# Mean over 8192 rows: two more row groups loaded as a pair, and a different split of one group between TensorE and VectorE

## The chip, the cores and the metric

The kernel runs on one core of one Trainium2 chip. A core has TensorE (matrix multiply, into PSUM banks), VectorE (called DVE in the profile), ScalarE (ACT), GpSimd (POOL), SyncE (SP, which here only issues transfers and waits), and sixteen DMA engines that move data between HBM and the on-chip SBUF. The metric is the device time of one execution in microseconds (us), lower being better. Before the change it was 628.19 us, the median of three runs that went from 628.13 to 628.68.

## The reference

```python
def setup_inputs():
    return {"x": np.random.randn(8192, 8192).astype(np.float32)}

def reference(x):
    return np.mean(x, axis=0)
```

The input is 8192 x 8192 float32, 268.4 MB, and each element is needed once. The output is 8192 means, one per column.

## The kernel before, in words

The rows are cut into 64 groups of 128 (`G = 64`, `P = 128`); a group is a tile of 128 partitions x 8192 columns, 4 MiB. The columns are spoken of in 16 blocks of `F = 512`. A sum over rows has two parts: adding groups to each other, partition by partition, which VectorE does into the running tile `acc`, and adding the 128 partitions of a tile, which TensorE does at the end by a matmul with a column of 1/8192 (`ones`).

SBUF holds six tiles (`bufs`): four that receive loads, `both` (the sum of a pair) and `acc`. All loads go through `load` (L75), which issues a transfer on SyncE's queue in program order. A load waits until the last reader of its buffer is done. In addition every load with an even number waits for the two loads that are seven and eight places before it (L78).

The first six groups come in two large loads. Then a loop (L120 to L133) takes groups in pairs: one load of two groups (8 MiB), one add of the pair's two tiles into `both`, one add of `both` to `acc`. The pair's two buffers are free again after the first of those adds. It runs for groups 6 to 55. A second loop (L135 to L138) takes groups 56 to 59 singly: a load of 4 MiB, and one add of the tile to `acc`, after which its buffer is free. The buffer of group g is number (g + 2) modulo 4.

Where an add has to wait for a load as well as for the add ahead of it, a no-op on ScalarE or GpSimd (`add`, L94 to L109, chosen by the count of adds so far) waits for both, and the add waits for the no-op.

The last four groups are split. Of group 60, VectorE adds 14 blocks to `acc` (the last two were added earlier, by GpSimd, from `early`). Of group 61 it adds some blocks, and TensorE sums the others straight from the loaded tile. Group 62 goes to TensorE, but for three blocks that GpSimd adds to `acc` (L147 to L149). Group 63 arrives in four pieces, blocks 4 to 7, 0 to 3, 14 to 15 and 8, and TensorE sums them as they land; its blocks 9 to 13 came early and were added by GpSimd.

TensorE's work is the list `sums` (L154 to L181), in the order in which it is written. `blocks(row, lo, hi)` puts one matmul per block on it. Block i goes to PSUM bank i // 4 and to quarter i % 4 of its partitions, so that four matmuls with different quarters can run side by side. `spread` cuts a range of columns over the four quarters, into the PSUM tiles `wide`, `two` and `last`. At the end ScalarE and VectorE copy the sums to SBUF (L209 to L214), and five small stores write the output.

Of the kernel before, what the change touches and what calls it, by code (L numbers as in the profile page):

```python
# [9 lines left out]
def kernel(  # L10
# [2 lines left out]
    x: bass.AP,  # L13
    out: bass.AP,
):

    nc = tc.nc
    f32 = mybir.dt.float32
    M, N = x.shape  # L40
# [3 lines left out]
    G = M // P  # L44
# [8 lines left out]
    acc = bufs[:, U - 1, :]  # L53
# [21 lines left out]
    def load(dst, src):  # L75
        ins = tc.keep_in_program_order(nc.sync.dma_start(out=dst, in_=src)).ins  # L76
        k = len(loads)
        over = loads[k - 8:k - 6] if k >= 8 and k % 2 == 0 else []  # L78
        tc.declare_no_dep(ins, group="loads", keep=over, reason="the reader of the buffer waited")
        for o in over:  # L80
            tc.add_manual_dep(ins, o.name, sync, reason="covers the next load too")
        tc.add_to_no_dep_group("loads", ins)
        loads.append(ins)
        return ins

    def rows(g, n=1):
        return x[g * P:(g + n) * P, :]

    def load_rows(g, u, n):
        return load(bufs[:, u:u + n, :], rows(g, n).rearrange("(p j) c -> p j c", j=n))  # L90
# [3 lines left out]
    def add(dst, a, b, dmas):  # L94

        ins = nc.vector.tensor_add(out=dst, in0=a, in1=b).ins  # L96
        if dmas and adds:
            waiter = nc.scalar if len(adds) % 8 > 1 else nc.gpsimd
            nop = joins[waiter] = tc.keep_in_program_order(waiter.nop()).ins  # L99
            for o in dmas + adds[-1:]:  # L100
                tc.add_manual_dep(nop, o.name, sync, reason="the no-op waits")
            for group in ("loads", "adds"):
                tc.declare_no_dep(ins, group=group, reason="the no-op waited")
            tc.add_manual_dep(ins, nop.name, sync, reason="waits for both at once")
        elif adds:
            tc.declare_no_dep(ins, group="loads", reason="the add ahead waited")
        tc.declare_no_dep(ins, group="early", reason="the no-op waited, or the add behind it")
        tc.add_to_no_dep_group("adds", ins)
        adds.append(ins)  # L109
# [7 lines left out]
    tc.keep_in_program_order(nc.scalar.copy(out=warm[:], in_=ones[:]))  # L117
    ahead = []
    g = 6
    while g < G - 8:  # L120
        u = (g + 2) % 4
        dma = load_rows(g, u, 2)
        add(both, bufs[:, u, :], bufs[:, u + 1, :], [dma])
        add(acc, acc, both, ahead)
        ahead = []
        if g in (24, 32):
            lo, hi = (0, 4) if g == 24 else (4, 7)
            cols = slice((9 + lo) * F, (9 + hi) * F)
            ins = tc.keep_in_program_order(nc.gpsimd.tensor_add(  # L129
                out=acc[:, cols], in0=acc[:, cols], in1=early[:, lo * F:hi * F])).ins  # L130
            tc.add_to_no_dep_group("early", ins)
            ahead = [ins]
        g += 2  # L133

    while g < G - 4:  # L135
        row = bufs[:, (g + 2) % 4, :]
        add(acc, acc, row, [load(row, rows(g))])
        g += 1  # L138
    for lo, hi, loaded in [(0, 14, 14), (7, 16, 16)]:
        row = bufs[:, (g + 2) % 4, :]  # L140
        dma = load(row[:, :loaded * F], rows(g)[:, :loaded * F])
        cols = slice(lo * F, hi * F)
        add(acc[:, cols], acc[:, cols], row[:, cols], [dma])
        g += 1
    r61, r62, r63 = [bufs[:, (g + 1 + j) % 4, :] for j in range(3)]
# [10 lines left out]
    def blocks(row, lo, hi):  # L156
        for i in range(lo, hi):
            sums.append((banks[i // 4], i % 4, 0, row[:, i * F:(i + 1) * F]))
# [5 lines left out]
                at = lo * F + q * n + c  # L164
                sums.append((dst, q, c, row[:, at:at + min(F, n - c)]))

    blocks(acc, 2, 5)
    blocks(acc, 0, 2)
    blocks(r61, 0, 7)
    blocks(acc, 5, 8)  # L170
    blocks(r62, 0, 8)
    spread(wide, acc, 9, 14, slice(1))
    blocks(r63, 4, 8)
# [83 lines left out]
```

## Time and profile before

| What | Value |
|---|---|
| Device time, median of three runs | 628.19 us |
| Profiled execution: span from first to last instruction | 626.39 us |
| Device time above that span | 1.80 us |
| VectorE busy | 529.3 us (85%) |
| TensorE busy | 13.3 us, all of it after 609.9 us |
| Read from HBM | 268.44 MB, mean 429 GB/s over the span |
| Median time from issue to landing of 27 of the loads | 29.9 us |

The profiled execution's own time is known by its span; the device time of the runs holds something more around it. In the views, times are microseconds from the start of the span. A timeline's line has the start, the duration, the engine, the line of the kernel, the operation with its output and input, how many instructions were merged into the line, and in brackets how long the engine was idle before it and what ended that. A line of groups has the busy time, the mean duration of one in ns, and the idle time before them with its releasers. The chain of waits is followed back from the last instruction, and printed in order of time: start, duration, and who held it. PEld is TensorE's loading of weights, which goes on beside its matmuls; a float32 matmul leaves two weight loads and two matmuls in the trace.

### The profile page before, as it was taken

The numbers are of one execution on the slowest core, as the hardware profiler recorded it, in microseconds if no ns is written. First come the engines' busy times: TensorE is split into PE (matmuls) and PEld (weight loads), VectorE is DVE, ScalarE is ACT, GpSimd is POOL, SyncE is SP. The second block draws the span as 40 slices with busy tenths as digits, with TensorE's granted clock in tenths as the row PEclk, the third lists the DMA queues.
The fourth block names the chain that finished last, engine by engine and source line by source line (L and its number), as shares of the span: only waits on it lengthen the run. The fifth ranks groups of instructions, "written<-read, shape, count | busy, mean of one in ns | idle before, by whom it ended". The sixth has DMA issues, their size and how long they took to land.

```text
span 626.4 us, 484 instructions
## 1 busy us (share of the span) xinstructions
PE 13.3 (2%) x126; PEld 4.0 (1%) x126; DVE 529.3 (85%) x60; ACT 3.7 (1%) x6; POOL 12.0 (2%) x10
## 2 busy tenths in 40 slices
PE   0000000000000000000000000000000000000008
PEld 0000000000000000000000000000000000000002
DVE  0028999998888998889998899888898888999992
ACT  0000000000000000000000000000000000000001
POOL 0000000000000000020000200000000000000002
PEclk9999999999999999999999999999999999999999
DMA  8999999999999999999999999999999999999997
GB/s 372 465 402 428 459 410 460 402 469 402 469 402 469 402 469 402 469 402 469 402 465 406 439 431 427 444 410 460 402 469 402 469 402 469 402 435 435 419 435 305
DMA packets 5930, 268.50 MB, mean 429 GB/s; under 512 B 660, under 2 KB 668, under 8 KB 1064
## 3 DMA queue, kind: packets, MB, share of 16 engines
q1 hardware_dynamic: 5912, 268.46, 99.3%
q8 instruction: 1, 0.02, 0.0%
q10 hardware_dynamic: 16, 0.01, 0.0%
q14 instruction: 1, 0.01, 0.0%
HBM read 268.44 MB, written 0.03 MB: 429 GB/s over the span
## 4 chain that ended last, share of the span: by engine, by line
DMA 59%; DVE 30%; another core or an unknown queue 10%; issue 0%; SPq 0%; ACTq 0%; PE 0%; POOL 0%; POOLq 0%
DMA bufs<-in_x_dram 59%; DVE bufs L96 30%; SPq L76 0%; ACTq L99 0%; PE last L183 0%; DVE tail L214 0%; POOL ready L61 0%; POOL ones L58 0%; POOLq L99 0%; POOLq L241 0%
## 5 line engine op out<-in xcount | busy, mean ns | idle before, releaser
L96 DVE TENSOR_TENSOR bufs<-bufs 128x8192 f32<-128x8192 f32 (+3 forms) x59 | 529.0, 8966 | 85.9 <-DMA bufs<-in_x_dram 43.0
L183 PE MATMUL bank<-bufs,ones 128*32 128x512 f32 x62 | 10.0, 716 | 610.3 <-DVE bufs L96 610.0
L129 POOL TENSOR_TENSOR bufs<-bufs,early 128x2048 f32<-128x2048 f32 (+1 forms) x2 | 7.9, 3954 | 348.5 <-DVE bufs L96 348.5
L148 POOL TENSOR_TENSOR bufs<-bufs 128x1024 f32<-128x1024 f32 (+1 forms) x2 | 3.6, 1824 | 258.9 <-DMA bufs<-in_x_dram 258.9
L214 DVE COPY tail<-last 128x128 f32<-128x128 f32 x1 | 0.3, 291 | 8.8 <-PE last L183 8.8
L183 PEld LDWEIGHTS bank<-bufs,ones 128*32 128x32 f32 x62 | 2.2, 121 | 616.4 <-issue 614.5
L198 ACT COPY bufs<-bank 128x512 f32<-128x512 f32 x2 | 1.2, 586 | 617.9 <-PE bank L183 617.9
L183 PE MATMUL wide<-bufs,ones 128*32 128x512 f32 (+1 forms) x32 | 2.5, 432 | 0.0
L117 ACT ACT_TABLE_LOAD x1 | 1.3, 1283 | 0.7 <-PEq L241 0.7
L183 PE MATMUL two<-bufs,ones 128*32 128x256 f32 x16 | 1.2, 380 | 0.0
L183 PEld LDWEIGHTS wide<-bufs,ones 128*32 128x32 f32 x32 | 1.0, 110 | 1.8 <-issue 1.8
L183 PE MATMUL last<-bufs,ones 128*32 128x128 f32 x16 | 0.8, 279 | 0.1
L198 ACT COPY bufs<-wide 128x640 f32<-128x640 f32 x1 | 0.7, 692 | 1.1 <-PE wide L183 1.1
L183 PEld LDWEIGHTS last<-bufs,ones 128*32 128x32 f32 x16 | 0.4, 109 | 1.2 <-issue 0.6
L183 PEld LDWEIGHTS two<-bufs,ones 128*32 128x32 f32 x16 | 0.4, 109 | 0.1
L198 ACT COPY bufs<-two 128x256 f32<-128x256 f32 x1 | 0.4, 372 | 0.1
L117 ACT COPY warm<-ones 128x32 f32<-128x32 f32 x1 | 0.2, 217 | 0.0
L61 POOL TENSOR_TENSOR ready<-ones 128x1 f32<-128x1 f32 x1 | 0.2, 193 | 0.1
L58 POOL MEMSET ones<- 128x32 f32 x1 | 0.1, 125 | 0.3 <-POOLq L241 0.3
L241 POOL MEMSET const-float32-0.0<- 128x1 f32 x1 | 0.1, 98 | 0.2 <-issue 0.2
L241 POOL MEMSET const-bfloat16-1.0<- 128x1 bf16 x1 | 0.1, 102 | 0.0
L241 POOL MEMSET const-uint8-127<- 128x1 uint8 x1 | 0.1, 102 | 0.0
(1 smaller groups left out, 0.1 us busy)
## 6 DMA issues: line engine op xcount, KB each, us to landing
bufs<-in_x_dram SPq DMA_DIRECT2D x6, 4096.0 KB, 20.4
bufs<-in_x_dram SPq DMA_DIRECT2D x1, 3584.0 KB
bufs<-in_x_dram SPq DMA_DIRECT2D x2, 1024.0 KB, 18.7
early<-in_x_dram SPq DMA_DIRECT2D x1, 1280.0 KB
early<-in_x_dram SPq DMA_DIRECT2D x1, 512.0 KB
bufs<-in_x_dram SPq DMA_DIRECT2D x1, 512.0 KB, 19.4
bufs<-in_x_dram SPq DMA_DIRECT2D x27, 29.9
bufs<-in_x_dram SPq DMA_DIRECT2D x1, 256.0 KB, 19.7
```

Of the source, the lines that this page charges most:

```text
L58: nc.gpsimd.memset(ones[:], 1.0 / M)
L61: nc.gpsimd.tensor_add(out=ready[:], in0=ones[:, 0:1], in1=ones[:, 1:2]))
L96: ins = nc.vector.tensor_add(out=dst, in0=a, in1=b).ins
L117: tc.keep_in_program_order(nc.scalar.copy(out=warm[:], in_=ones[:]))
L129: ins = tc.keep_in_program_order(nc.gpsimd.tensor_add(out=acc[:, cols], in0=acc[:, cols], in1=early[:, lo * F:hi * F])).ins
L148: joined = tc.keep_in_program_order(nc.gpsimd.tensor_add(out=acc[:, cols], in0=acc[:, cols], in1=r62[:, cols])).ins
L183: summed = tc.keep_in_program_order(nc.tensor.matmul(out=dst[32 * q:32 * q + 32, c:c + cols.shape[1]], lhsT=ones[:], rhs=cols, start=all(( ...
L198: return tc.keep_in_program_order(nc.scalar.copy(out=dst, in_=src)).ins
L214: ended = nc.vector.tensor_copy(out=tail[:], in_=last[:]).ins
L241: nc = _bacc.Bacc("TRN2", target_bir_lowering=False, num_devices=1)
```

## The change

The loop over pairs runs for one pair more, groups 56 and 57, so the loop over single groups has only 58 and 59 left. Of group 61, VectorE now adds blocks 8 to 15 (before 7 to 15) and TensorE sums blocks 0 to 7 (before 0 to 6). TensorE's list begins with blocks 0 to 7 of `acc` and then blocks 0 to 7 of group 61, where before it had blocks 2 to 4 and 0 to 1 of `acc`, blocks 0 to 6 of group 61, and blocks 5 to 7 of `acc`. Some empty lines are gone, which moves line numbers by 22.

```diff
-    while g < G - 8:
+    while g < G - 6:
         u = (g + 2) % 4
         dma = load_rows(g, u, 2)
         add(both, bufs[:, u, :], bufs[:, u + 1, :], [dma])
...
-    for lo, hi, loaded in [(0, 14, 14), (7, 16, 16)]:
+    for lo, hi, loaded in [(0, 14, 14), (8, 16, 16)]:
         row = bufs[:, (g + 2) % 4, :]
         dma = load(row[:, :loaded * F], rows(g)[:, :loaded * F])
         cols = slice(lo * F, hi * F)
...
-    blocks(acc, 2, 5)
-    blocks(acc, 0, 2)
-    blocks(r61, 0, 7)
-    blocks(acc, 5, 8)
+    blocks(acc, 0, 8)
+    blocks(r61, 0, 8)
     blocks(r62, 0, 8)
     spread(wide, acc, 9, 14, slice(1))
     blocks(r63, 4, 8)
```

## The prediction

> **What bounds the kernel now.** I read the page first (busy shares and DMA rows), then the chain of waits, VectorE's timeline over the last 110 us, the groups by form, and last the timeline of TensorE's weight loads.
>
> ```profile
> DMA  8999999999999999999999999999999999999997
> q1 hardware_dynamic: 5912, 268.46, 99.3%
> HBM read 268.44 MB, written 0.03 MB: 429 GB/s over the span
> ```
>
> The loads take 99.3% of the sixteen engines' time: the kernel is bound by reading x. It can gain from denser transfers or from a shorter end after the last byte, and lose by starving the queue or by lengthening the end.
>
> ```profile
> 593.41 8.70 DVE bufs L96
> 602.11 0.02 issue
> 602.13 0.33 SPq L76
> ...
> 603.45 19.74 DMA bufs<-in_x_dram
> 623.19 0.04 issue
> 623.23 0.47 PE last L183 x8
> ```
>
> The chain's end: the add of group 59 frees the buffer for group 63 (602.11), SyncE issues 63 in four pieces, the last lands 19.74 us later, and eight short matmuls close the sum at 623.23. Those 19.74 us are mostly queueing: groups 61 and 62 are ahead. So the landing sets the end, not the add.
>
> ```profile
> 530.16 17.42 DVE L96 TENSOR_TENSOR bufs<-bufs 128x8192 f32<-128x8192 f32 x2 [1.93 <-POOLq L99]
> 549.50 65.39 DVE L96 TENSOR_TENSOR bufs<-bufs 128x8192 f32<-128x8192 f32 x8 [1.93 <-ACTq L99]
> ```
>
> Pairs arrive every 549.50 - 530.16 = 19.34 us and cost VectorE 17.42, so it idles 1.93 per pair. From 549.50 on (pair 54/55, then single groups) it never waits, until 614.89.
>
> ```profile
> L96 DVE TENSOR_TENSOR bufs<-bufs 128x8192 f32<-128x8192 f32 x55 | 482.0, 8763 | 40.5 <-ACTq L99 30.6 <-POOLq L99 8.2
> L96 DVE TENSOR_TENSOR bufs<-bufs 128x7168 f32<-128x7168 f32 x1 | 7.6, 7625 | 0.1
> L96 DVE TENSOR_TENSOR bufs<-bufs 128x4608 f32<-128x4608 f32 x1 | 5.0, 4957 | 0.1
> ```
>
> The last two forms are the adds of groups 60 and 61: (7625 - 4957) / 2560 = 1.042 ns a column.
>
> ```profile
> 609.95 0.24 PEld L183 LDWEIGHTS bank<-bufs,ones 128*32 128x32 f32 x8 [609.95 <-issue]
> 610.85 0.18 PEld L183 LDWEIGHTS bank<-bufs,ones 128*32 128x32 f32 x1 [0.66 <-issue]
> ...
> 613.41 0.16 PEld L183 LDWEIGHTS bank<-bufs,ones 128*32 128x32 f32 x5 [0.68 <-issue]
> 613.88 0.12 PEld L183 LDWEIGHTS bank<-bufs,ones 128*32 128x32 f32 x3 [0.31 <-issue]
> ...
> 616.28 0.16 PEld L183 LDWEIGHTS bank<-bufs,ones 128*32 128x32 f32 x8 [1.19 <-DMA bufs<-in_x_dram]
> 616.73 0.13 PEld L183 LDWEIGHTS bank<-bufs,ones 128*32 128x32 f32 x4 [0.30 <-issue]
> ...
> 622.52 0.16 PEld L183 LDWEIGHTS two<-bufs,ones 128*32 128x32 f32 x8
> 623.23 0.16 PEld L183 LDWEIGHTS last<-bufs,ones 128*32 128x32 f32 x8 [0.55 <-DMA bufs<-in_x_dram]
> ```
>
> This view matters most. Each 512-column matmul leaves two weight loads, and four run at once, in steps. TensorE starts at 609.98 (after the add of group 60), steps by 0.855 us until 613.41, then by 0.43: its clock doubled after 3.43 us. The profile's clock row reads 1.00 throughout, so the clock must be read from the steps. Group 62 lands at 616.28; its eight blocks take four steps (1.72 us). From there TensorE runs without a gap into 622.52, where the piece (14,16) of group 63 has just landed. Those eight short records take two steps, to about 622.97, and then it waits for the last landing at 623.23. **So the landing-bound end hides only 0.26 us of lateness of TensorE's final run.**
>
> **The change, part by part.**
>
> *Pair load of 56/57.* SyncE loses one issue of 0.33 us, in a queue that sits waiting for VectorE. Transfer: a pair takes 19.34 us per 8 MiB. Between pair 54/55 (549.50) and group 62 (616.28) there are 27.5 MiB in 66.78 us, or 19.43 per 8 MiB. One more pair saves 0.09, say 0.10 us of every later landing: group 62 at 616.18, the last at 623.13.
>
> *VectorE.* The same two 8192-column adds, one no-op join fewer. Before, group 57's add ended at 584.52 (the chain's single adds start every 8.80 us). Now the pair lands at 549.50 + 19.34 = 568.84, the usual 1.93 of idle returns, and its adds end at 568.84 + 17.42 = 586.26. Everything behind is 1.74 us later, including the end of group 60's add and so TensorE's start: 609.98 + 1.74 = 611.72. Group 61's add has 512 columns less: -0.53 us, ending at 614.89 + 1.74 - 0.53 = 616.10.
>
> *Buffers.* Groups 60 and 61 now wait for the pair's first add (568.84 + 8.71 = 577.55); their transfer starts near 588, when 59 has landed. Group 62 waits for 58's add (593.31 + 1.74 = 595.05; transfer from about 606). Group 63 waits for 59's add (603.85; transfer from about 616). Each has 10 us or more in hand; cost nothing. Without that cover, it is microsecond for microsecond.
>
> *SyncE's second wait.* One load fewer moves the even-numbered loads' wait for the transfers seven and eight back by one place. Those landed long before (the nearest, 59, lands near 588 and is wanted at 605): nothing, and 0.03 us on SyncE. The number of adds is the same, so ScalarE and GpSimd keep the same no-ops.
>
> *GpSimd's two adds* need group 62 (616.18) and group 61's add (616.10): 0.08 us to spare. They run 3.61 us from 616.49. TensorE wants them at 620.92, so 0.8 us of cover is left.
>
> *TensorE.* One block more, and the eight blocks of acc now need only group 60's add, so none waits for group 61's. But the start is 1.74 us later. Sixteen blocks make 32 records, eight steps of four: 6.84 us at the slow step, 3.44 at the fast one. If the clock doubles c us after the start, they end at 611.72 + c + (8 - c/0.855) x 0.43 = 615.16 + 0.497c. Against group 62's landing this is late by 0.497c - 1.02. TensorE runs on without a gap from there, 0.26 is absorbed before the last landing, and landings are 0.10 earlier. The end moves by **0.497c - 1.38 us, but not below -0.10**.
>
> What is c? The row gives 3.43, from 609.98 to 613.41, but one doubling doesn't tell what it is tied to. Low end: tied to the time, not to the start; it comes at 613.41 again, c = 1.69, end -0.10. High end: the later start misses one stretch of 3.43 and must sit through the next, c = 6.86, end +2.03. In between, the row itself: +0.32. The trace's record of the granted clock has full speed from 613.47 to 627.13, and 13.65 is four times 3.41. I read this as decisions at the ends of stretches of 3.41, with a start that happened to lie within 0.1 us of the beginning of one. Then 3.43 is the short end when a full busy stretch is needed, and anything up to 6.86 is as likely; if a partly busy stretch suffices, shorter ones occur too. I take the middle of the ends, (1.69 + 6.86) / 2 = 4.3: late by 1.12, **end +0.76 us**. If TensorE did have a perfect cover, as before, this term would be zero.
>
> The Trainium skill, "TensorE: Matmul & The Clock Gate", Part 1 (the HAM clock gate), speaks against the change: it says the clock goes to full speed after a busy window of 3413 ns that is "free-running — it doesn't reset when your kernel starts". By it, with only full windows counting, c lies between 3.41 and 6.83, in the middle 5.12: +1.16 us, 629.35 in all. The one doubling seen here agrees with it but can't show that the phase varies.
>
> **Sum.** Transfers -0.10, TensorE's lateness behind its slack +0.86 (1.12 - 0.26): +0.76 on the profiled span of 626.39, so 627.15. The median of the runs, 628.19, lies 1.80 above that span, which I take as constant: 628.95, rounded to 629.0.
>
> **Rivals.**
>
> *TensorE catches up* (c under about 3.1): steps of 0.43 from early on, group 62's blocks start at 616.2 on landing, and the end is set by the last transfer: 628.1 to 628.35. For it: 613.41 would be early enough. Against: at the same pace as before (3.43) it is already 0.69 late. Chance 0.20.
>
> *The slow clock lasts into group 62's blocks* (c over 5.3): the end moves more than 1.26 us, up to 2.03, giving 629.45 to 630.2, slower by over 0.2% (0.2%, or 1.26 us, is about what a measurement of this kernel can tell from no change). Place: the first six to eight steps after the start. For it: TensorE's work has no idle time before 622.5 in which to catch up. Against: it needs nearly a whole second stretch. Chance 0.26.
>
> *The buffer chain starves the queue*: if group 63's issue (about 605) slipped beyond 616, each microsecond would count. It needs VectorE 11 us later than worked out; nothing in its rows is so large. Some 630 or more; 0.02.
>
> *Faster by over 0.2%*: 1.26 us must come off transfers whose rows differ by 0.1 us, or off an end that begins only at 623.1. I see no place for it: 0.03.
>
> **How the numbers follow.** The forecast (+0.3 to +1.26, c from 3.4 to 5.3, 628.5 to 629.45) has 0.49; with the first rival, within 0.2% has 0.69. Slower: 0.26 + 0.02 = 0.28. Faster: 0.03. The range runs from just below the catch-up case, 628.0, to 630.0, near the high end of c; 0.2 is left outside, for c near its ends, for the 0.55 us by which the three runs differ, and for the last two cases.
>
> **What would show it.** VectorE: idle of 1.9 us near 567, the last four adds in a row to about 616.1. TensorE: start at 611.7, slow steps of 0.855, their number the measure of c, no wait at group 62. Landings: about 0.1 us earlier. Last matmuls: no wait on the DMA before them if I am right, a wait if the first rival is. It would be wrong if four records no longer ran at once with the new order of blocks, or if VectorE's start of the pair were later than 568.9.

## The result

| Kernel | Median (us) | Lowest to highest | Runs |
|---|---|---|---|
| before | 628.29 | 628.11 to 628.68 | 17 |
| changed | 629.33 | 628.52 to 630.67 | 17 |

The ratio is 1.0019, with a 95% interval of 1.0012 to 1.0025: slower by 0.12 to 0.25%, about 1.2 us. The forecast was 629.0, range 628.0 to 630.0. The runs of the changed kernel spread over 2.15 us, those of before over 0.57.

### The profile after

The profiled execution of the changed kernel has a span of 628.0 us. In it the first large load landed 0.81 us later than in the profile of before (VectorE's first add starts at 43.80, before 42.99), which shifts everything behind by about 0.8 us; two more profiles of the same kernel, below, do not have this shift. So positions are compared as distances: from the start of pair 54/55's add, or from group 62's landing (0.21 us ahead of the start of GpSimd's add, as before: 616.28 and 616.49).

The end of the chain of waits of the changed kernel (start, duration, who held it):

```profile
604.80 7.63 DVE bufs L74
612.43 0.14 issue
612.57 7.25 PE bank L159 x48
619.82 0.86 PE wide L159 x8
...
624.34 0.43 PE two L159 x8
624.77 0.26 PE last L159 x8
625.03 0.02 issue
625.05 0.29 DVE tail L190
```

Before, the last 20 us of the chain were a load. Now they are TensorE's matmuls, without a gap, behind the add of group 60. The loads are no longer what ends last. (In both profiles the chain stops at VectorE's copy of `tail`; the stores behind it are taken up below, with the table of the three profiles.)

VectorE, GpSimd and TensorE's weight loads in the timeline of the same run:

```profile
550.33 17.42 DVE L74 TENSOR_TENSOR bufs<-bufs 128x8192 f32<-128x8192 f32 x2 [1.94 <-ACTq L77]
569.68 47.27 DVE L74 TENSOR_TENSOR bufs<-bufs 128x8192 f32<-128x8192 f32 x6 [1.93 <-ACTq L77]
612.54 0.23 PEld L159 LDWEIGHTS bank<-bufs,ones 128*32 128x32 f32 x8 [612.54 <-issue]
613.39 0.23 PEld L159 LDWEIGHTS bank<-bufs,ones 128*32 128x32 f32 x4 [0.62 <-issue]
...
615.95 0.23 PEld L159 LDWEIGHTS bank<-bufs,ones 128*32 128x32 f32 x4 [0.62 <-issue]
616.62 0.14 PEld L159 LDWEIGHTS bank<-bufs,ones 128*32 128x32 f32 x4 [0.44 <-issue]
617.05 0.14 PEld L159 LDWEIGHTS bank<-bufs,ones 128*32 128x32 f32 x4 [0.29 <-issue]
617.26 3.62 POOL L126 TENSOR_TENSOR bufs<-bufs 128x1024 f32<-128x1024 f32 x2 [258.88 <-DMA bufs<-in_x_dram]
...
624.37 0.35 PEld L159 LDWEIGHTS last<-bufs,ones 128*32 128x32 f32 x8
```

VectorE idles 1.93 us ahead of pair 56/57, as worked out, and TensorE starts at 612.57, 62.24 after pair 54/55's add (before: 609.98 - 549.50 = 60.48; 1.76 more). The steps are 0.855 us until 616.4, so c is 3.86: the trace's clock record has full speed from 616.43, and 616.43 - 612.57 = 3.86. Group 62 lands at 617.05, but its first block starts with the ninth step, at 617.91, 0.86 us late. The last line has no wait for a load: the records for block 8 of group 63 follow straight on, where before they waited 0.55 us for the landing.

### The profile page after: what moved, and what is told of

It reads as the page before. It is cut to its first block, busy times and chain, and to the rows that moved or that the text cites. A ratio compares the mean times of both kernels' runs of the same rounds, so it can differ in the third digit from the quotient of the medians.

```text
span 628.0 us, 487 instructions
## 1 busy us (share of the span) xinstructions
PE 12.4 (2%) x128; PEld 4.5 (1%) x128; DVE 528.8 (84%) x60; ACT 3.7 (1%) x6; POOL 12.1 (2%) x10
## 4 chain that ended last, share of the span: by engine, by line
DMA 57%; DVE 31%; another core or an unknown queue 10%; PE 2%; issue 0%; ACTq 0%; POOLq 0%; POOL 0%
DMA bufs<-in_x_dram 57%; DVE bufs L74 31%; PE bank L159 1%; PE wide L159 0%; PE two L159 0%; PE last L159 0%; ACTq L77 0%; POOLq L77 0%; DVE tail L190 0%; POOL ready L39 0%; POOL ones L36 0%; POOLq L217 0%
```

## The experiments

The theory: with the pair, TensorE starts 1.74 us later; how long its clock then stays at the slow step is not tied to its start, so it is late for group 62 by a varying amount, and everything from there to the end has, by the prediction, only 0.26 us in hand. Rivals: the new order and the extra block cost the time; the pair's transfer or VectorE's later adds do; or the slow stretch has a fixed length and the spread has another cause.

### One part of the change at a time

Split and order alone:

```diff
-    while g < G - 6:
+    while g < G - 8:
```

> The change without the pair: groups 56 to 59 come singly again, the split of group 61 (eight and eight) and the new order of TensorE's list stay. Theory of the late start: TensorE starts near 610.0 in the span again, sixteen blocks end at 613.42 + 0.497c, at most 0.54 us after group 62's landing for c up to 6.86 and so at most 0.28 us beyond the slack; median within 0.2 us of the kernel before. Rival, the new order or the extra block costs the time: about 1.1 us slower than before, as the whole change.

Measured: 628.48 (627.97 to 628.77, and one run at 630.66; 11 runs), before 628.31 (24 runs); ratio 1.0006, interval 0.9997 to 1.0015.

The pair alone, on the kernel before:

```diff
-    while g < G - 8:
+    while g < G - 6:
```

> The change without the new split: 56/57 come as a pair, VectorE adds nine blocks of group 61, TensorE's list is in its old order. Theory of the late start: TensorE starts 1.74 us later than before, and block 7 of acc must wait for group 61's add, which now ends near 616.6 instead of 614.9; as slow as the whole change or a little slower, +0.8 to +1.6 us in the median, runs spread over 1.5 us or more. Rival, the new order or the extra block costs the time: within 0.2 us of the kernel before.

Measured: 629.80 (629.49 to 630.26, 8 runs); ratio 1.0025, interval 1.0014 to 1.0035. The timeline of the first, with split and order alone:

```profile
613.63 0.22 PEld L159 LDWEIGHTS bank<-bufs,ones 128*32 128x32 f32 x4 [0.63 <-issue]
614.15 0.14 PEld L159 LDWEIGHTS bank<-bufs,ones 128*32 128x32 f32 x4 [0.30 <-issue]
...
616.54 0.16 PEld L159 LDWEIGHTS bank<-bufs,ones 128*32 128x32 f32 x8 [1.82 <-DMA bufs<-in_x_dram]
...
623.42 0.16 PEld L159 LDWEIGHTS last<-bufs,ones 128*32 128x32 f32 x8 [0.47 <-DMA bufs<-in_x_dram]
```

and of the second, with the pair alone:

```profile
612.05 7.84 PE L183 MATMUL bank<-bufs,ones 128*32 128x512 f32 x46 [612.05 <-DVE bufs L96]
...
617.02 0.25 PEld L183 LDWEIGHTS bank<-bufs,ones 128*32 128x32 f32 x5 [0.49 <-DVE bufs L96]
617.11 3.63 POOL L148 TENSOR_TENSOR bufs<-bufs 128x1024 f32<-128x1024 f32 x2 [259.28 <-DVE bufs L96]
...
624.38 0.42 PEld L183 LDWEIGHTS last<-bufs,ones 128*32 128x32 f32 x8
```

Without the pair TensorE waits for group 62 and for the last landing, as before. With it neither wait is left, whatever the split. So the pair carries the cost, and the new order and extra block carry none that can be measured (the interval leaves room for up to 0.9 us). In the second, GpSimd and block 7 of acc wait for VectorE, which the new split avoids; that it is worth something beside the pair is not shown, since the intervals overlap.

### Taking away the slow clock, first try

Idle matmuls ahead of TensorE's list, 24 on group 60 and 20 (on the changed kernel) or 16 (on the kernel before) on group 61, so that the clock is up when acc is ready:

```diff
+    junk = psp.tile([P, F], f32, name="junk")
+    def fill(row, count):
+        for i in range(count):
+            q = i % 4
+            tc.keep_in_program_order(nc.tensor.matmul(
+                out=junk[32 * q:32 * q + 32, :], lhsT=ones[:],
+                rhs=row[:, (i % 8) * F:(i % 8 + 1) * F], start=True, stop=True,
+                tile_position=(0, 32 * q), skip_group_check=True))
+    fill(bufs[:, 2, :], 24)
+    fill(r61, 20)
     for n, (dst, q, c, cols) in enumerate(sums):
```

> The changed kernel with idle work for TensorE ahead of its first useful block: 24 matmuls on group 60 and 20 on group 61, 512 columns each, into a PSUM tile that nobody reads. Nothing else differs. Theory of the slow clock: TensorE is at full speed when acc comes near 611.7, its sixteen blocks take eight steps of 0.43 (3.4 us) and end by 615.2, before group 62 lands; the last landing sets the end: 0.1 us faster than before, 1.1 us faster than the changed kernel, and the runs spread no more than those of before. Rival, the lateness comes from the pair's transfer or from VectorE's later adds: no gain, +1.1 us against before.

> The kernel before with the same idle work for TensorE, 24 matmuls on group 60 and 16 on group 61. Theory of the slow clock: the kernel before has enough slack for its slow steps, so nothing is gained, within 0.1 us of before; the difference to the changed kernel with idle work is the pair's transfer alone, 0.1 us. Rival, the idle work itself speeds the end or disturbs the loads: more than 0.3 us faster or slower than before.

Measured: 629.91 on the changed kernel (629.53 to 631.63, 5 runs; ratio 1.0037, interval 1.0023 to 1.0050) and 629.56 on the kernel before (629.13 to 630.20, 11 runs; ratio 1.0020, interval 1.0011 to 1.0028). Both expectations failed. The timeline of the first:

```profile
615.29 0.13 PEld L170 LDWEIGHTS bank<-bufs,ones 128*32 128x32 f32 x4 [0.30 <-issue]
617.70 0.16 PEld L170 LDWEIGHTS bank<-bufs,ones 128*32 128x32 f32 x8 [2.27 <-DMA bufs<-in_x_dram]
...
624.53 0.16 PEld L170 LDWEIGHTS last<-bufs,ones 128*32 128x32 f32 x8 [0.43 <-DMA bufs<-in_x_dram]
```

TensorE's part came out as the theory says: fast steps, the sixteen blocks done by 616.3, waits for both landings. But the landings themselves were late: 617.49 for group 62 on the kernel before, where it had been 616.28. The packets of the trace show one candidate: a 16 KB packet of the instruction queue that took 1.08 us of one DMA engine. It came at 622.56 in the profile of before and at 622.64 in that of the changed kernel, when the loads were nearly done; with the idle matmuls it came at 613.20 and 614.22, amid the loads. What else the idle matmuls do is read SBUF for some 12 us.

### Many instructions, little work

The kernel before, with 40 matmuls of 32 columns instead:

```diff
+    r60 = bufs[:, 2, :]
+    for i in range(40):
+        q = i % 4
+        ... nc.tensor.matmul(out=junk[32 * q:32 * q + 32, :32], lhsT=ones[:],
+                rhs=r60[:, i % 8 * F:i % 8 * F + 32], ...)
```

> The kernel before with 40 matmuls of only 32 columns on group 60 when it has landed, ten for each quarter, into a PSUM tile that nobody reads: as many more TensorE instructions as the idle work had, but only some 2 us of TensorE time, over long before acc is ready. In both kernels with idle work one 16 KB transfer of the instruction queue came at 613 to 614, amid the loads, took 1.08 us of one DMA engine, and the landings behind it were about 1.1 us later; without idle work it comes at 622.6. If more TensorE instructions bring that transfer forward and it costs the landings: the transfer comes before 618, group 62 lands about 1.1 us later, +1.1 us in the median. If the heavy reading by TensorE's idle work delayed the loads: transfer at 622.6, no change from before.

Measured: 629.58 (629.23 to 629.82, 11 runs), before 628.30 (27 runs); ratio 1.0019, interval 1.0010 to 1.0028. The timeline:

```profile
597.10 1.29 PE L186 MATMUL junk<-bufs,ones 128*32 128x32 f32 x80 [597.10 <-DMA bufs<-in_x_dram]
...
616.48 1.92 PE L190 MATMUL bank<-bufs,ones 128*32 128x512 f32 x16 [0.27 <-DMA bufs<-in_x_dram]
...
622.86 0.16 PEld L190 LDWEIGHTS bank<-bufs,ones 128*32 128x32 f32 x8 [1.50 <-DMA bufs<-in_x_dram]
...
624.72 0.16 PEld L190 LDWEIGHTS last<-bufs,ones 128*32 128x32 f32 x8 [0.47 <-DMA bufs<-in_x_dram]
```

The instruction packet came at 618.62, not before 618 as expected. Group 62, ahead of it, landed in time (616.48, with this run's first add 0.16 late); the pieces behind it were about 1.4 us late, as the wait of 1.50 shows. The 1.29 us of TensorE work was over 20 us earlier, so it is not the reading of SBUF. The trace's landing records, sixteen for each load, show where the delay sits: up to the piece that landed at 618.92 the last record comes 0.01 or 0.02 us behind the fifteenth, and in each of the three pieces after the packet a single record is 1.37 to 1.42 us behind the other fifteen. In the first try's profiles the same step, from 0.03 to 1.29 and 1.39, lies between groups 61 and 62, on either side of the packet. So more TensorE instructions bring that packet forward, and amid the loads it costs the landings behind it more than 1 us. The first try had swapped one delay for another. Why that is 0.1 to 0.3 us more than the packet's own 1.08 is not shown.

### Warming with three instructions

On the changed kernel, three matmuls, all in quarter 0:

```diff
+    for i in range(3):
+        q = 0
+        ... nc.tensor.matmul(out=junk[32 * q:32 * q + 32, :512], lhsT=ones[:],
+                rhs=r61[:, i % 8 * F:i % 8 * F + 512], ...)
```

> The changed kernel with only three matmuls more, 512 columns each, all in one quarter, on group 61 as soon as it lands near 606.2: six steps, 5.1 us at the slow pace, to about 611.3, with next to no more instructions. Theory of the slow clock: the clock has doubled by 613 at the latest, the sixteen blocks end before 616.2, the last landing sets the end, 0.1 us faster than before with the narrow spread of before (if the instruction transfer stays behind the loads). If one quarter of the array is not enough work to raise the clock: as slow as the changed kernel, +1.1 us.

Measured: two clusters, four runs from 628.31 to 628.55 and seven from 630.16 to 630.76 (median 630.24, ratio 1.0023, interval 1.0013 to 1.0033). The profile is of a run at 628.52:

```profile
609.95 0.17 PEld L161 LDWEIGHTS junk<-bufs,ones 128*32 128x32 f32 x1 [0.68 <-issue]
611.67 0.20 PEld L165 LDWEIGHTS bank<-bufs,ones 128*32 128x32 f32 x8 [1.54 <-DVE bufs L74]
612.47 0.12 PEld L165 LDWEIGHTS bank<-bufs,ones 128*32 128x32 f32 x4 [0.60 <-issue]
612.89 0.12 PEld L165 LDWEIGHTS bank<-bufs,ones 128*32 128x32 f32 x4 [0.31 <-issue]
...
616.23 0.16 PEld L165 LDWEIGHTS bank<-bufs,ones 128*32 128x32 f32 x8 [1.50 <-DMA bufs<-in_x_dram]
...
623.14 0.16 PEld L165 LDWEIGHTS last<-bufs,ones 128*32 128x32 f32 x8 [0.47 <-DMA bufs<-in_x_dram]
```

Here is the test that the first try was meant to be. The same pair, the same late start at 611.67, but the clock doubles at 612.4, 0.73 us in, and all the cost is gone: group 62's blocks start on landing, the last landing sets the end, and the span is 626.37 against 626.39 before. Since the pair and VectorE's later adds are in this run too, it speaks against the rival that they cost the time by themselves. To see the upper cluster I ran it twice more:

> The changed kernel with three matmuls in one quarter once more, for a profile of one of its slow executions (its times fell into two clusters, 628.3 to 628.6 and 630.2 to 630.8). If work in one quarter counts too little for the clock, the profile of a slow one shows steps of 0.855 far into the sixteen blocks, group 62's blocks late by up to 2 us, and the landings in place. If the three more instructions bring the instruction transfer forward amid group 63's pieces, the sixteen blocks end in time and the last landing is 1 to 2 us late.

> The same kernel again, since one execution in three or so falls into its fast cluster: late clock or late landings, whichever the one before shows, should be seen again if the time is near 630.3, and neither if it is near 628.4.

Both fell in or near the lower one, 628.77 and 628.37, with clock and landings in place (last matmuls at 623.40 and 623.07; the clock record of the second has full speed from 609.67, while the three matmuls still ran). So the upper cluster was not seen in a profile, and its cause stays open.

### Group 61 first

```diff
-    blocks(acc, 0, 8)
     blocks(r61, 0, 8)
+    blocks(acc, 0, 8)
```

> The changed kernel with group 61's eight blocks ahead of acc's eight in TensorE's list. Group 61 lands near 606.2, so TensorE starts 5.5 us earlier and works off half of the sixteen blocks before acc is ready, then idles about 2 us, and about 1 us again before group 62. If the clock doubles only after a whole busy stretch of about 3.4 us, neither piece is long enough, group 62's blocks begin at the slow step, and the end is 1.3 to 3 us later than before. If the clock counts time from TensorE's first work, or a partly busy stretch suffices, it is at full speed by 612: as fast as before, or 0.1 us faster.

> The changed kernel with group 61 first once more (its times fell into 628.4 to 628.8 and 629.7 to 630.2). Theory of the slow clock: an execution near 628.5 has group 62's blocks at steps of 0.43 from their landing on; one near 630 begins them at 0.855, steps slowly for 3 us or more behind group 62's landing, and has its last matmuls 1.3 to 1.8 us late with the landings in place. Rival, late landings: steps of 0.43, and the last landing late.

Measured: two clusters again, seven runs from 628.39 to 628.84 and four from 629.74 to 630.22 (median 628.82; ratio 1.0013, interval 1.0004 to 1.0022). The further run took 628.80. Its timeline:

```profile
607.02 0.23 PEld L159 LDWEIGHTS bank<-bufs,ones 128*32 128x32 f32 x8 [607.02 <-issue]
...
612.18 0.20 PEld L159 LDWEIGHTS bank<-bufs,ones 128*32 128x32 f32 x8 [3.22 <-DVE bufs L74]
613.04 0.20 PEld L159 LDWEIGHTS bank<-bufs,ones 128*32 128x32 f32 x4 [0.66 <-issue]
613.89 0.20 PEld L159 LDWEIGHTS bank<-bufs,ones 128*32 128x32 f32 x4 [0.66 <-issue]
616.73 0.16 PEld L159 LDWEIGHTS bank<-bufs,ones 128*32 128x32 f32 x8 [2.64 <-DMA bufs<-in_x_dram]
617.18 0.13 PEld L159 LDWEIGHTS bank<-bufs,ones 128*32 128x32 f32 x4 [0.30 <-issue]
```

Neither of my two outcomes held alone. All of the first sixteen blocks ran at slow steps, group 61's and then acc's, and the clock still came up in time for group 62 (the record has 615.74, as the second piece ended). So it is not time since the first work that counts (8.7 us here), and a stretch of some 3.5 us of work can be enough. The other cluster is told by the mean granted clock of each run: 0.997 in the four from 629.74 on, 0.999 or 1.000 in the seven others. A stretch of 3.4 us at half speed lowers the mean by 1.7 / 628 = 0.0027, so each of the four fits one such lapse after an early rise; a profile of it was not taken.

### The changed kernel twice more

> The changed kernel once more, for another profile of it. If the slow stretch after TensorE's start has no fixed length, this one has another c than 3.86, and the distance from group 62's landing to the start of its first block follows 0.497c - 1.02. If the length is fixed, c is 3.86 again and the difference between runs comes from elsewhere.

> The changed kernel a third time. c was 3.86 and 5.33 in its first two profiles; a third value between 3 and 6.9 with group 62's first block late by 0.497c - 1.02 against its landing speaks for a doubling that is not tied to TensorE's start. An equal c would speak against it.

Measured: 630.02 and 629.45. GpSimd's and TensorE's lines of the first:

```profile
616.05 0.22 PEld L159 LDWEIGHTS bank<-bufs,ones 128*32 128x32 f32 x4 [0.63 <-issue]
616.48 3.60 POOL L126 TENSOR_TENSOR bufs<-bufs 128x1024 f32<-128x1024 f32 x2 [258.86 <-DMA bufs<-in_x_dram]
616.91 0.23 PEld L159 LDWEIGHTS bank<-bufs,ones 128*32 128x32 f32 x4 [0.63 <-issue]
617.45 0.14 PEld L159 LDWEIGHTS bank<-bufs,ones 128*32 128x32 f32 x4 [0.32 <-issue]
617.88 0.13 PEld L159 LDWEIGHTS bank<-bufs,ones 128*32 128x32 f32 x4 [0.29 <-issue]
```

Starts, clock records and lateness of the three profiles (landing is GpSimd's start less 0.21; the last column is from there to the first record of the closing matmuls, 6.95 us before):

| Profile | Start | Clock up | c | Landing | Group 62's first block | Late | 0.497c - 1.02 | Landing to closing |
|---|---|---|---|---|---|---|---|---|
| first | 612.57 | 616.43 | 3.86 | 617.05 | 617.91 | 0.86 | 0.90 | 7.53 |
| second | 611.81 | 617.14 | 5.33 | 616.27 | 617.88 | 1.61 | 1.63 | 8.28 |
| third | 611.59 | 616.36 | 4.77 | 616.05 | 617.39 | 1.34 | 1.35 | 8.00 |

The slow stretch has no fixed length, and the lateness follows it to 0.04 us. The last column is 6.95 + late - 0.26 to within 0.03 us: at the closing matmuls the slack is 0.26 in all three.

At the end of the span it is not. From the landing to there it is 10.92, 11.68 and 11.40 us in the three profiles, against 10.11 before: longer by 0.81, 1.57 and 1.29, which is the lateness less 0.05. The place is SyncE's stores, in the profile of before

```profile
622.43 1.26 SPq L201 DMA_DIRECT2D out_dram<-bufs  x2
624.04 0.50 SPq L201 DMA_DIRECT2D out_dram<-tail  x1
```

and in the first one of the changed kernel:

```profile
624.04 1.26 SPq L177 DMA_DIRECT2D out_dram<-bufs  x2
625.37 0.50 SPq L177 DMA_DIRECT2D out_dram<-tail  x1
```

The first store waits for ScalarE's copy of `wide`, whose sums do not need the last landing. From its issue to the end of the span it is 3.96 us before and 3.94 here, and 3.93 to 3.97 in thirteen of the fourteen profiles; the one with forty small matmuls has 5.32, and there the second store had to wait for late blocks. The last store's issue, in contrast, is 2.35 us ahead of the end before and 2.60 here. So TensorE's lateness reaches the end through the first stores, and the last landing hid nearly none of it. That the last store queues behind the two ahead of it is a likely reason (its first packet comes 0.86 us after that of the store ahead in the profile of before, 0.81 to 0.83 in the three); no run here tests it.

## Why the prediction was right

**Direction and mechanism** held: a late start of TensorE, a slow stretch of varying length, no gap in which to catch up, the end set by TensorE instead of the last landing. The three profiles carry each step; the pair alone shows the pair as the cause, and the three warming matmuls show the clock, by the three profiles in or near their lower cluster. Seven of their eleven runs lie above the changed kernel's median, and that is not explained.

**VectorE.** Its shift was worked out as 1.74 us and measured as 1.76; its last add ends at 569.68 + 47.27 = 616.95, which is 66.62 after pair 54/55's add, against 66.60 (616.10 - 549.50) worked out.

**The transfer.** From pair 54/55's add to group 62's landing: 66.78 us before, 66.72, 66.70 and 66.69 in the three profiles. The pair saves 0.06 to 0.09 us of the 0.10 taken.

**The mis-sized term is the slack.** The prediction lets 0.26 us of TensorE's lateness vanish behind the last landing. It does so at the closing matmuls, but at the end of the span only 0.05 us vanished in the three profiles, because the end follows SyncE's first stores. That makes the forecast 0.21 us too short, over half of the 0.38 us between it and the measured median; another 0.10 is that the kernel before has 628.29 in 17 runs and not the 628.19 of three.

**c** was taken as 4.3, the middle between a low end of 1.69 and a high end of 6.86. The medians lie 1.04 us apart, which with a slack of 0.05 and landings 0.08 earlier is c = (1.04 + 1.02 + 0.05 + 0.08) / 0.497 = 4.4; the ratio, 1.2 us, gives 4.7. So the size was near, but in part by luck, since the low end was wrong: it stood for a doubling near 613.41 whatever the start, and it came at 616.36 to 617.14 in the three profiles, with c at 3.86 to 5.33 (5.06 with the pair alone). Over c from 3.4 to 6.9 the end would vary by 1.7 us, which with the 0.57 of the kernel before is about the 2.15 us of spread; this is an estimate, since the profiles reach only from 3.86 to 5.33. The row of before, 3.43, was near the short end, as I had suspected; but the middle between it and twice it, 5.1, would have been too long for the median.

The Trainium skill, "TensorE: Matmul & The Clock Gate", Part 1, has the clock at full speed after a busy window of 3413 ns that is free-running. The estimate worked out from it in the prediction, c between 3.41 and 6.83, holds the c of all four profiles with the pair and without added or moved work (3.86 to 5.33). That its 629.35 lies nearer to the measured 629.33 than my forecast is luck: with the slack at 0.05 its c of 5.12 gives 1.4 us over the kernel before, 629.7. One limit is left open here: in the run with group 61 first that has a clock record, the clock rose at the end of a piece of work of 3.6 us, hardly longer than a window.

**The rivals.** Catching up was not seen: the lowest runs of the changed kernel (628.52 and 628.59) lie above the 628.35 that this rival allowed, and none of them was profiled. The slow clock never reached group 62's blocks: in the three profiles it was over 0.74 to 1.48 us before the first of them. The condition of that rival, c over 5.3, was met by one profile, 5.33 at 630.02. Eight of the seventeen runs lie above its 629.45, but a time alone doesn't tell c: the profiled run at 630.08 is one of them, with a c of 3.86 and loads that began 0.81 us late. The buffer chain did not starve the queue: group 62 landed on time relative to the pair.

**What I missed.** That the start of the loads varies, by 0.81 us between two profiles (in the later one a single landing record is 0.58 to 0.65 us behind the other fifteen in each of the last six loads), so a single profile's positions can be compared only as distances. And that adding TensorE instructions isn't free for the loads.

## What to carry to other kernels

Where an engine's last run has no idle time, look for how much of a delay is hidden on each path to the end: here the last landing hid 0.26 us of the closing matmuls, but the stores fed by earlier sums only 0.05. Any delay beyond that goes to the end in full, however idle the engine was for the 610 us before. TensorE, which wakes only at the end of this kernel, worked its first 3.4 to 5.3 us at half speed in the five profiles of the kernel before, the changed kernel and the pair alone, so its start must be early enough for the long case, not for the one that the profile happens to show; one profile with a spread of runs beside it tells whether the margin is there. Before a transfer is made denser, ask what its later landing does to whoever consumed the first half early: here 0.1 us of transfer was bought with 1.74 us of start.

## What the runs showed of the hardware

- The instruction queue's 16 KB packet took 1.08 us of one DMA engine. In the profile of before it came at 622.6, when the loads were nearly done; with 40 to 44 more TensorE matmuls it came at 613 to 619, one of the sixteen landing records of each load behind it was 1.2 to 1.4 us late, and the kernel before was 1.3 us slower.
- Work in a single quarter of TensorE's array went before a rise of the clock at 609.67, 3.2 us after it began, in one profile, so full use of the array was not needed for that rise. Whether it always suffices is open, with the upper cluster.
- The clock can fall behind an idle stretch: with the idle matmuls on the kernel before it fell at 607.7, after 2.26 us of idleness that had ended at 606.39, and rose again at 611.1.
- Left open: the cluster of 630.2 to 630.8 with three warming matmuls, and the single run at 630.66 with the split alone.
